# PSUM tiles per stage, and a norm's operands made by quarters, in a two-layer decoder trunk

## The chip, the cores and the metric

The kernel runs on one core of a Trainium2 chip. The time is device microseconds (us) of one execution; the median of several runs is given. The core has engines with a queue each, worked off in order: TensorE (PE in the profile; its weight loads are PEld), VectorE (DVE), ScalarE (ACT), GpSimd (POOL) and SyncE (SP), which issues DMAs. Matmuls write to PSUM, eight banks of 512 fp32 columns over 128 partitions; DVE and ACT read it from there.

## The reference

x has 512 positions and 1024 channels, fp32. Two layers follow each other, each of three sublayers:

```python
x = x + 0.5 * swiglu(rmsnorm(x, ln_ffn1[l]), w_ffn1_gu[l], w_ffn1_down[l])
h = rmsnorm(x, ln_mix[l])
u_pool, q, k, v, gate_logits = jnp.split(h @ w_in[l], splits, axis=-1)
a = pool_mixer(u_pool, pool_w[l], pool_scale[l]) @ w_pool_branch[l]
b = swa_sink_attention(rope(norm(q)), rope(norm(k)), v, sinks[l]) @ w_attn_branch[l]
g_pool, g_attn = jnp.split(jax.nn.sigmoid(gate_logits), 2, axis=-1)
x = x + (g_pool * a + g_attn * b) @ w_out[l]
x = x + 0.5 * swiglu(rmsnorm(x, ln_ffn2[l]), w_ffn2_gu[l], w_ffn2_down[l])
```

(The calls of norm and rope are shortened here.) swiglu(h) is (silu(h Wg) * (h Wu)) Wdown with 2816 hidden columns. The mixer has causal window means of 2, 4, 8 and 16 positions beside attention with 8 query and 2 key heads over a window of 128 positions.

## The kernel before, in words

**Precision.** Every fp32 product is made of three matmuls on fp32r halves: each operand is split into a high half (a cast on ACT) and a low half (source minus high half, on DVE), and `term` issues high x high, high x low, low x high. `split` does this for activations, `Weights` for weights: a weight tile is loaded to `raw`, then `wh` is cast on ACT and `wl` subtracted on DVE. Each call of `W.prep()` after a consumed tile makes the next `wl` (three tiles ahead) and `wh` (four ahead), and sums of weight tiles (five ahead). All engines run in the order of the program text; nothing is reordered by a scheduler.

**Strassen blocks.** A FFN is worked off in three groups of hidden columns (384 + 384, 512 + 512, 512 + 512; the narrow group comes first in the very first FFN and second in the others, so the last one is always wide). Each group has one or two blocks for gate and up, and then one product with the down weights, `down`. Block and down are a Strassen-like scheme (`strassen`, L504) of seven products, named a11, s1, s2, a12, s3, s4, a22. Each adds up in one of three two-bank PSUM tiles: A takes a11, s2, s3 and a22, C takes s1 and s4, Dd takes a12. So A holds a running sum that is read after each of its four products before the next one may add to it. The order is `ORDER` = a11, s1, s2, a12, s3, s4, a22, in the block after a norm `FIRST` = a11, s1, a12, s2, s3, s4, a22. In `down` (L704), the step after each product updates a quarter of x (or two, for a22: row by row) with one DVE operation `x<-mm,x`. Each product has two weight tiles (c = 0, 1) and two halves of rows (q); the weights of s2 and s4 are sums of others.

**Operands of down.** `turned` (L606) transposes the block's results on PE into a fourth two-bank PSUM tile, `turn` (named pt in the profile), and from it makes with ACT and DVE the operands `op` of the seven products, by way of `fa`, `fb` and `fc`. The second block's part t = 1 is turned right after the block; the part t = 0 is held back in `turns` and turned by `flush`, the step after a11 of down. Its result is the operand of a12 and the last term of `fa`, from which a22's operand is made.

**The norm's operand.** The next sublayer's operand is x scaled by the gain (the factor of each row is put on the result), transposed. `Norm.feed(k, pt)` (L375) transposes 128 channels of all 512 positions into one bank, and makes the halves: for a FFN (`halves`) four plain quarters B11, B12, B21, B22 and combinations T1 to T4, for the mixer the plain halves alone. In the last down of a FFN channels 0 to 511 are fed during and after a22 (`mid`), channels 512 to 1023 and the combinations by closures in `pend`, which `due()` runs at fixed points of the next sublayer's first products.

**The mixer.** The tiles A, C and Dd are used bank by bank: `mm()` (L323) hands out the four banks of two of them in turn, for the u, gate and branch products (L1011, L1071); the third holds attention scores (`wide`). The two banks of `turn` take transposes (of heads, of probabilities) and the product with v. Attention, pooling and head norms are generators whose steps stand at fixed half tiles between the u and gate products (`side`, L1006). The gate tile's PSUM is read by `z<-mm,R` on DVE. The out product (L1088) runs over two halves of the channels (d) with four row blocks each.

A tile is the unit of the waits: this shows in the trace, where PE waits for the reader of another bank of the same two-bank tile.

Of the kernel before, what the change touches and what calls it, by code (L numbers as in the profile page):

```python
# [9 lines left out]
F32 = mybir.dt.float32  # L10
# [8 lines left out]
P = 128  # L19
L = 2  # L20
S = 512
# [7 lines left out]
PLACE = {B11: 0, T1: 1, B21: 2, B22: 3}  # L29
OF = {"a11": B11, "s1": T1, "s2": T2, "a12": B21, "s3": T3, "s4": B22, "a22": T4}  # L30
# [77 lines left out]
def trunk(ctx, tc, x0, xT, consts, vecs, rows, w_g4, w_g3, w_d8, w_d6, w_qkv, w_u, w_pool, w_gate, w_br, w_out, out):  # L108
# [6 lines left out]
    pa = pool("pa", 1, space=PSUM)  # L115
# [14 lines left out]
    two = [pa.tile([P, 2, S], F32, name=f"mm{i}") for i in range(3)]  # L130
    turn = pa.tile([P, 2, S], F32, name="pt")
    for _ in range(WARM):
        nc.tensor.matmul(turn[:, 1, :2 * P], warm[:, :P], warm, start=True, stop=True)
# [26 lines left out]
    class Weights:  # L160
# [3 lines left out]
        def __init__(self):  # L164
# [3 lines left out]
            for l in range(L):  # L168
                for f in range(2):
# [9 lines left out]
                    for gi, (at, group) in enumerate(groups(plain)):  # L179
# [9 lines left out]
                        if at:  # L189
                            w = w_d8[l, f, at // 1024]  # L190
                            self.block(lambda h, k, c, w=w: w[h, k, c], (CH, CH), ORDER)
                        else:
                            w = w_d6[l, f]
                            cols = slice(0, CH), slice(CH, 3 * S)
                            self.block(lambda h, k, c, w=w: w[h, k][:, cols[c]], (CH, S), ORDER)

# [149 lines left out]
    class Norm:  # L346
# [15 lines left out]
        def spare(self, j):  # L362
            if j not in self.more:
                self.more[j] = [xl.tile([P, 3 * HT], F32R, name=n, tag=f"{n}{j}") for n in ("th", "tl")]
            return self.more[j]

        def of(self, i, j, n=1):
            if i in PLACE:
                i = PLACE[i]
                return [t[:, i:i + n, j, :] for t in (self.h, self.l)]  # L370
            i -= T2
            return [t.rearrange("p (i t) -> p i t", t=HT)[:, i:i + n, :] for t in self.spare(j)]


        def feed(self, k, pt):  # L375
# [8 lines left out]
            if k < 4:  # L384
                self.keep[k] = xl.tile([P, S], F32, name="keep", tag=f"th{k}")
            xg = self.keep[k] if k < 4 else temp("xg")
            nc.scalar.activation(out=xg, in_=pt, func=AF.Copy, scale=g)
            if k < 4:
                split(*self.of(B11, k), halves(xg)[:, 0:1, :])
                self.first(k, xg)  # L390
            else:
                split(*self.of(B21, k - 4, 2), halves(xg))
                return xg

        def first(self, j, src, scale=None):
            d = temp("d")[:, :HT]
            nc.vector.tensor_tensor(out=d, in0=src[:, :HT], in1=src[:, HT:], op=ALU.subtract)
            split(*self.of(T1, j), halves(d), scale=scale)

        def others(self, j, src, xg, scale=None):  # L400

            t, u = temp("t23"), temp("t4")[:, :HT]
            if scale is None:
                nc.vector.tensor_tensor(out=t[:, HT:], in0=xg[:, HT:], in1=src[:, HT:], op=ALU.subtract)
            else:
                nc.vector.scalar_tensor_tensor(
                    out=t[:, HT:], in0=src[:, HT:], scalar=scale, in1=xg[:, HT:], op0=ALU.mult, op1=ALU.add
                )
            nc.vector.scalar_tensor_tensor(
                out=t[:, :HT], in0=src[:, :HT], scalar=-1.0 if scale is None else scale, in1=t[:, HT:],  # L410
                op0=ALU.mult, op1=ALU.subtract,
# [4 lines left out]
            split(*self.of(T2, j, 2), halves(t))  # L416
            split(*self.of(T4, j), halves(u))

        def split_plain(self, k, b12, src):
            g = self.gain[:, k:k + 1]  # L420
            self.opened()
            if k < 4:
                split(*self.of(B11, k), halves(src)[:, 0:1, :], scale=g)
                split(*(t[:, k:k + 1, :] for t in b12), halves(src)[:, 1:2, :], scale=g)
            else:
                split(*self.of(B21, k - 4, 2), halves(src), scale=g)
# [39 lines left out]
        def spread(self):  # L466
            pr = turn[:, 1, :]
# [5 lines left out]
        def terms(self, w):  # L473
            return pairs(w, [(self.h[:, k, :], self.l[:, k, :]) for k in range(KT)])
# [3 lines left out]
    roles = list(two)  # L478
    pend = []

    def due(n=1):
        for _ in range(n):
            if pend:
                pend.pop(0)()

    @with_exitstack
    def ffn(ctx, nm, nxt, last):
        op = ctx.enter_context(tc.tile_pool(name="op", bufs=3, reuse_waits="tile"))
# [15 lines left out]
        def strassen(order, n, sizes, operand, steps, mid={}):  # L504
# [31 lines left out]
            roles[:] = [Dd, C, A]  # L536
# [694 lines left out]
```

## Time and profile before

| | us |
|---|---|
| median of 3 runs (2042.04 to 2048.88) | 2044.02 |
| profiled execution, whole | 2051.07 |
| its span, first to last instruction | 2049.3 |
| PE busy | 1908.7 (93%) |
| DVE busy | 1461.9 (71%) |
| ACT busy | 1001.5 (49%) |
| mean granted clock of TensorE | 0.971 |

A row of the timeline reads: start, duration, engine, operation, out<-in by the program's names, shape, count, and in brackets the idle time of the engine before it and what ended it. Where a helper records all operations, all have one line (L96 here), so the names of the tiles tell them apart. In a name with several inputs, mm<-wh,op is a matmul into mm of the moving wh and the stationary op. The granted clock is the share of full speed that the throttle let TensorE have; it is either 1 or 0.5 at a time, so 0.96 over a stretch is half clock for 8% of it. Durations of matmuls are modelled and overlap; the distance between their starts is what they cost.

### The profile page before, as it was taken

The page shows a single profiled execution, that of the slowest core. Times are in us where ns is not written, and L with a number is a line of the kernel's source. Part 1 is how long each engine was busy: PE and PEld are TensorE (multiplying, and loading weights), DVE is VectorE, ACT ScalarE, POOL GpSimd, SP SyncE. Part 2 cuts the span into 40 slices and gives each one's busy share as a digit, 9 for nine tenths or more (in the row PEclk, how much of TensorE's full clock was granted, in tenths as well). Part 3 has the DMA queues.
Part 4 walks back from the last instruction along what each step waited for, and adds up shares of the span by engine and source line. Part 5 has one row for each costly group of instructions (what it writes and reads, how often), then busy time and mean ns, then how long its engine had stood idle before and what let it go on. Part 6 is the DMA issues. An engine that isn't in the chain of part 4 may idle for free.

```text
span 2049.3 us, 23932 instructions
## 1 busy us (share of the span) xinstructions
PE 1908.7 (93%) x8928; PEld 1590.7 (78%) x8928; DVE 1461.9 (71%) x1873; ACT 1001.5 (49%) x1457; POOL 124.8 (6%) x152
## 2 busy tenths in 40 slices
PE   9999999878999899999879999998789998999998
PEld 8887887766687678988758897877666786789886
DVE  7877878546454778777877877785555547787877
ACT  6555455344344555555555455553343445545553
POOL 0100100000000000110000111000000000001100
PEclk9999999989999999999989999999999999999999
DMA  7677774211124576676546677742212244666763
GB/s 231 176 210 189 187 188 135 88 62 62 62 83 103 135 178 166 171 213 173 152 117 170 157 182 188 198 144 90 70 51 73 83 103 134 175 161 174 210 180 93
DMA packets 87572, 292.81 MB, mean 143 GB/s; under 512 B 9856, under 2 KB 10112, under 8 KB 87456
## 3 DMA queue, kind: packets, MB, share of 16 engines
q1 hardware_dynamic: 67104, 223.47, 33.0%
q0 software_dynamic: 20208, 67.78, 19.6%
q8 instruction: 70, 1.15, 0.2%
q14 instruction: 46, 0.38, 0.1%
q10 hardware_dynamic: 144, 0.03, 0.0%
HBM read 289.15 MB, written 2.10 MB: 142 GB/s over the span
## 4 chain that ended last, share of the span: by engine, by line
PE 78%; DVE 13%; ACT 6%; issue 3%; DMA 0%; SPq 0%; DVEq 0%; ACTq 0%
PE mm L96 75%; PE pt L96 3%; DVE wl L96 3%; DVE sums L96 1%; ACT wh L96 1%; ACT s L96 1%; DVE x L96 1%; DVE tl L96 1%; ACT xgh L96 1%; ACT op L96 1%; DVE fb L96 1%; ACT sq L96 1%; DVE fa L96 1%; ACT th L96 1%; DVE r L96 1%
## 5 line engine op out<-in xcount | busy, mean ns | idle before, releaser
L96 ACT CAST wh<-raw 128x1024 fp32r<-128x1024 f32 (+3 forms) x443 | 434.4, 988 | 352.7 <-PE mm L96 279.6
L96 DVE TENSOR_TENSOR wl<-raw,wh 128x1024 fp32r<-128x1024 f32 (+3 forms) x443 | 504.5, 1145 | 114.3 <-PE mm L96 88.1
L96 PE MATMUL mm<-wh,op 128*128 128x512 f32 x1232 | 395.4, 399 | 0.0
L96 PE MATMUL mm<-wh,xgh 128*128 128x512 f32 (+2 forms) x904 | 334.8, 370 | 0.0
L96 PE MATMUL mm<-wl,xgh 128*128 128x512 f32 (+2 forms) x904 | 331.9, 367 | 2.0 <-DVE wl L96 1.9
L96 PE MATMUL mm<-wh,xgl 128*128 128x512 f32 (+2 forms) x904 | 331.7, 367 | 0.0
L96 PEld LDWEIGHTS mm<-wh,op 128*128 128x128 f32 x1232 | 237.5, 193 | 49.6
L96 PE MATMUL mm<-wl,op 128*128 128x512 f32 x616 | 244.8, 397 | 1.6 <-DVE wl L96 1.6
L96 PE MATMUL mm<-wl,th 128*128 128x512 f32 (+1 forms) x552 | 211.3, 383 | 14.1 <-DVE wl L96 14.1
L96 PE MATMUL mm<-wh,th 128*128 128x512 f32 (+1 forms) x552 | 211.3, 383 | 12.8 <-ACT u L96 12.5
L96 PE MATMUL mm<-wh,tl 128*128 128x512 f32 (+1 forms) x552 | 210.3, 381 | 0.0
L96 ACT CAST wh<-sums 128x1024 fp32r<-128x1024 f32 (+1 forms) x140 | 137.4, 981 | 129.3 <-DVE sums L96 116.5
L96 PEld LDWEIGHTS mm<-wl,xgh 128*128 128x128 f32 x904 | 170.7, 189 | 25.6 <-DVE wl L96 3.3
L96 DVE TENSOR_TENSOR wl<-sums,wh 128x1024 fp32r<-128x1024 f32 (+1 forms) x140 | 158.2, 1135 | 44.3 <-ACT wh L96 22.0
L96 PEld LDWEIGHTS mm<-wh,xgl 128*128 128x128 f32 x904 | 170.5, 189 | 22.9
L96 PEld LDWEIGHTS mm<-wh,xgh 128*128 128x128 f32 x904 | 170.8, 189 | 22.2
L96 PE MATMUL mm<-xgh,wh 128*128 128x512 f32 x320 | 137.4, 429 | 36.3 <-DVE tl L96 19.4
L96 POOL DMA_DIRECT2D raw<-in_w_g x92 | 79.4, 863 | 1474.0 <-DMA raw<-in_w_g 648.1
L96 PEld LDWEIGHTS mm<-wl,op 128*128 128x128 f32 x616 | 118.8, 193 | 27.5 <-DVE wl L96 3.3
L96 PE MATMUL mm<-xgl,wh 128*128 128x512 f32 x320 | 132.0, 412 | 0.0
L96 PE MATMUL mm<-xgh,wl 128*128 128x512 f32 x320 | 131.6, 411 | 0.0
L96 PEld LDWEIGHTS mm<-wl,th 128*128 128x128 f32 x552 | 106.8, 193 | 31.9 <-DVE wl L96 15.6
(228 smaller groups left out, 2538.6 us busy)
## 6 DMA issues: line engine op xcount, KB each, us to landing
raw<-in_w_g SPq DMA_DIRECT2D x160, 512.0 KB, 4.7
raw<-in_w_d SPq DMA_DIRECT2D x100, 512.0 KB, 4.4
raw<-in_w_g POOLq DMA_DIRECT2D x64, 512.0 KB, 5.9
raw<-in_w_g SPq DMA_DIRECT2D x77, 384.0 KB, 4.0
raw<-in_w_d POOLq DMA_DIRECT2D x40, 512.0 KB, 5.5
raw<-in_w_gate SPq DMA_DIRECT2D x32, 512.0 KB, 3.3
raw<-in_w_g POOLq DMA_DIRECT2D x28, 384.0 KB, 5.3
raw<-in_w_br SPq DMA_DIRECT2D x16, 512.0 KB, 3.3
```

The source lines that it names most:

```text
L96: return lambda *args, **kw: self.tc.keep_in_program_order(call(*args, **kw))
```

## The change

PSUM is now allocated by each stage: a FFN opens three two-bank tiles and `turn` as before, the mixer opens four single banks for `mm()`, one two-bank tile for the scores and two single banks in place of `turn`. The physical banks follow each other as before (`order_`).

In `down` the order is a11, s1, s2, a12, s4, s3, a22, and `flush` runs after s1 instead of after a11. In `turned`, `fa` and `fb` of the second block's part t = 1 read `fc`, the copy in SBUF, instead of PSUM. The operands have fixed places (`AT`) instead of rotating ones.

`feed(q, i, pt)` now makes a quarter-sized piece: 256 channels (q of 4) of 256 positions (i of 2), with eight transposes. ACT scales it in two operations out of PSUM into SBUF, and everything else reads SBUF. In the last down pieces (0, 0) and (1, 0) are fed in s4, (0, 1) and (1, 1) in s3, (2, 1) and (3, 1) in a22; (2, 0) and (3, 0) follow in the next sublayer's first product. In the mixer's out product six of the eight are fed within its second half, whose last two weight tiles are worked off row block by row block (blocks 2 and 3 first), with both their `W.prep()` calls at the end. The mixer's operand lies in another layout, by which u and gate read it in two runs of 256 columns. Its first products are reordered: half of u, half of k and v, the rest of u, the rest of k and v.

```diff
+DOWN = ("a11", "s1", "s2", "a12", "s4", "s3", "a22")
 FIRST = ("a11", "s1", "a12", "s2", "s3", "s4", "a22")
...
+AT = {"a11": 0, "s1": 1, "s2": 2, "s3": 0, "a12": 1, "s4": 2, "a22": 1}
...
-    two = [pa.tile([P, 2, S], F32, name=f"mm{i}") for i in range(3)]
-    turn = pa.tile([P, 2, S], F32, name="pt")
...
+        def feed(self, q, i, pt):
 
             self.opened()
-            for b in range(NB):
-                nc.tensor.transpose(pt[:, b * P:(b + 1) * P], x[:, b, k * P:(k + 1) * P], ident)
-            g = self.gain[:, k:k + 1]
+            for k in range(2):
+                for b in range(2):
+                    at = k * HT + b * P
+                    nc.tensor.transpose(
+                        pt[:, at:at + P], x[:, 2 * i + b, (2 * q + k) * P:(2 * q + k + 1) * P], ident
+                    )
...
+            def scaled(xg):
+                for k in range(2):
+                    cols, n = slice(k * HT, (k + 1) * HT), 2 * q + k
+                    nc.scalar.activation(out=xg[:, cols], in_=pt[:, cols], func=AF.Copy, scale=self.gain[:, n:n + 1])
+                return xg
+
             if not self.halves:
-                split(self.h[:, k, :], self.l[:, k, :], pt, scale=g)
+                split(*(t[:, q, i].rearrange("p k t -> p (k t)") for t in (self.h, self.l)), scaled(temp("xg")))
                 return
...
+            j = q % 2
+            if q < 2 and i == 0:
+                self.keep[0, j] = scaled(self.place(0, 2, j, F32))
+                split(*self.both(B11, j), self.keep[0, j])
+            elif q < 2:
+                self.keep[1, j] = scaled(self.place(0, 0, j, F32))
+                d = temp("d")
+                nc.vector.tensor_tensor(out=d, in0=self.keep[0, j], in1=self.keep[1, j], op=ALU.subtract)
+                split(*self.both(T1, j), d)
+            elif i == 1:
+                xg = scaled(temp("xg"))
+                split(*self.both(B22, j), xg)
+                self.keep[2, j] = t = self.place(1, 0, j, F32)
+                nc.vector.tensor_tensor(out=t, in0=xg, in1=self.keep[1, j], op=ALU.subtract)
+                split(*self.both(T3, j), t)
             else:
...
+                xg, t, u = scaled(temp("xg")), temp("t2"), temp("t4")
+                split(*self.both(B21, j), xg)
+                nc.vector.scalar_tensor_tensor(
+                    out=t, in0=self.keep[0, j], scalar=-1.0, in1=self.keep[2, j], op0=ALU.mult, op1=ALU.subtract
+                )
+                split(*self.both(T2, j), t)
+                nc.vector.scalar_tensor_tensor(out=u, in0=t, scalar=-1.0, in1=xg, op0=ALU.mult, op1=ALU.subtract)
+                split(*self.both(T4, j), u)
...
         def terms(self, w):
-            return pairs(w, [(self.h[:, k, :], self.l[:, k, :]) for k in range(KT)])
...
+            return pairs(w, [[t[:, k // 2, :, k % 2, :] for t in (self.h, self.l)] for k in range(KT)])
...
+        pf = ctx.enter_context(tc.tile_pool(name="pf", bufs=1, space=PSUM, reuse_waits="tile"))
+        three = [pf.tile([P, 2, S], F32, name=f"mm{i}") for i in range(3)]
+        turn = pf.tile([P, 2, S], F32, name="pt")
+        roles = [three[i] for i in order_]
...
-                nc.vector.scalar_tensor_tensor(
-                    out=f["a"], in0=f["a"], scalar=-1.0, in1=pt, op0=ALU.mult, op1=ALU.subtract
-                )
                 f["c"] = fp.tile([P, 2, S], F32, name="fc")[:, :, :n]
                 nc.scalar.copy(out=f["c"], in_=pt)
+                nc.vector.scalar_tensor_tensor(
+                    out=f["a"], in0=f["a"], scalar=-1.0, in1=f["c"], op0=ALU.mult, op1=ALU.subtract
+                )
                 made("s2", f["a"], n)
-                nc.vector.tensor_tensor(out=f["b"], in0=pt, in1=f["b"], op=ALU.subtract)
+                nc.vector.tensor_tensor(out=f["b"], in0=f["c"], in1=f["b"], op=ALU.subtract)
...
-            def a11(pt):
-                add(0, 0, 0.5)(pt)
-                return flush
+            a11 = add(0, 0, 0.5)
 
             def s1(pt):
                 add(1, 1, -0.5)(pt)
                 made("s3", f["b"], n)
+                return flush
...
-                A, _, Dd = roles
-                mid["a22", 0, 1] = lambda: [nxt.feed(i, Dd[:, i, :]) for i in range(2)]
-                mid["a22", 1, 1] = lambda: [nxt.feed(2 + i, turn[:, i, :]) for i in range(2)]
-                pend.extend(stages(nxt, [A[:, 0, :], A[:, 1, :], turn[:, 0, :], turn[:, 1, :]]))
+                Dd = roles[2]
+                for i, (kind, q, t) in enumerate((("s4", 0, 0), ("s3", 0, 1), ("a22", 2, 1))):
+                    for k in range(2):
+                        bank = (Dd, turn)[k][:, 0, :]
+                        mid[kind, k, 1] = lambda q=q + k, t=t, bank=bank: nxt.feed(q, t, bank)
+                pend.extend((lambda bank, q=q: nxt.feed(q, 0, bank)) for q in (2, 3))
...
-                        mid = {("a11", 0, 1): lambda: due(2), ("a11", 1, 1): lambda: due(2), ("s1", 0, 1): due,
-                               ("s1", 1, 1): due, ("a12", 0, 1): due, ("a12", 1, 1): due}
+                        mid = {("a11", k, 1): lambda bank=bank: due(bank[:, 0, :]) for k, bank in ((0, turn), (1, roles[2]))}
...
+        pm = ctx.enter_context(tc.tile_pool(name="pm", bufs=1, space=PSUM, reuse_waits="tile"))
+        ring = {}
+        for i in range(3):
+            n = order_.index(i)
+            if n == 2:
+                wide = pm.tile([P, 2, S], F32, name="sc")
+            else:
+                ring.update((2 - 2 * n + j, pm.tile([P, S], F32, name=f"mm{n}{j}")) for j in range(2))
+        side_bank = [pm.tile([P, S], F32, name=n) for n in ("pt_tp", "pt_pv")]
+        used = [0]
+
+        def mm():
+            used[0] += 1
+            return ring[(used[0] - 1) % 4]
...
-            pt = turn[:, b // 2, :]
+            pt = side_bank[b // 2]
...
-                pk = turn[:, 1, :]
+                pk = side_bank[1]
...
-        for h in range(2):
+
+        def begun(h):
             for i in range(2):
                 for k, t in enumerate(nm.terms(w[i])[4 * h:4 * h + 4]):
                     term(late[i], 4 * h + k, KT, *t)
-                if h == 0:
-                    due(2)
+                if h:
+                    W.prep()
                 else:
-                    if i == 0:
-                        nm.sums()
-                    W.prep()
+                    due(side_bank[i])
+
+        begun(0)
...
+                w_ = W.take("qkv")
...
+                        kt, cols = per * c + k, slice(k * width, (k + 1) * width)
+                        rows = slice(b % 2 * P, (b % 2 + 1) * P)
+                        term(
+                            pts[b], kt, KT, *(t[:, kt // 2, b // 2, kt % 2, rows] for t in (nm.h, nm.l)),
+                            w_[0][:, cols], w_[1][:, cols],
+                        )
+                    if not q and c == 1 and b == 1:
+                        nm.spread(side_bank[1])
                         for i in range(2):
                             pooled(i, late[i])
+                if not q and c == 0:
+                    nm.sums()
+                    praw = temp("praw")
+                    nc.sync.dma_start(out=praw, in_=w_pool[l])
+                    begun(1)
                 if c + 1 < KT // per:
                     W.prep()
-                if not q and c == 0:
-                    praw = temp("praw")
-                    nc.sync.dma_start(out=praw, in_=w_pool[l])
                 if q and c == 1:
                     side(-2)
...
+        sides = [[mm() for _ in range(NB)], [wide[:, 0, :], wide[:, 1, :]]]
+        sides[1] += sides[0][:2]
+        feeds = iter([(q, i) for i in range(2) for q in range(2)] + [(q, 1) for q in (2, 3)])
...
+            for c in range(KT // 2 - 2 * d):
...
+                    part(d, b, c, w)
+                    if d and b % 2:
+                        nxt.feed(*next(feeds), side_bank[b // 2])
                 W.prep()
...
+            if d == 0:
+                for b in range(NB):
+                    added(d, b)
+        w = [W.take("out") for _ in range(2)]
+        for i in (1, 0):
+            for b in (2 * i, 2 * i + 1):
+                for c in range(2):
+                    part(1, b, 2 + c, w[c])
+                if i == 0:
+                    if b == 0:
+                        for n in (2, 3):
+                            added(1, n)
+                    nxt.feed(*next(feeds), side_bank[b])
+        for n in (0, 1):
+            added(1, n)
+        pend.extend((lambda bank, q=q: nxt.feed(q, 0, bank)) for q in (2, 3))
+        W.prep()
+        W.prep()
...
```

More of the change, by code (lines that the diff above doesn't have):

```diff
@@ L128, in trunk @@
     nc.vector.tensor_copy(out=onesr, in_=ones)
-    two = [pa.tile([P, 2, S], F32, name=f"mm{i}") for i in range(3)]
-    turn = pa.tile([P, 2, S], F32, name="pt")
-    for _ in range(WARM):
-        nc.tensor.matmul(turn[:, 1, :2 * P], warm[:, :P], warm, start=True, stop=True)
+    with tc.tile_pool(name="pw", bufs=1, space=PSUM, reuse_waits="tile") as pw:
+        cold = pw.tile([P, S], F32, name="cold")
+        for _ in range(WARM):
+            nc.tensor.matmul(cold[:, :2 * P], warm[:, :P], warm, start=True, stop=True)
     nc.scalar.activation(out=sp.tile([P, 1], F32, name="warm"), in_=ones[:, 0:1], func=AF.Silu)
@@ L375, in feed, with place, slot @@
-        def feed(self, k, pt):
-            self.opened()
-            for b in range(NB):
-                nc.tensor.transpose(pt[:, b * P:(b + 1) * P], x[:, b, k * P:(k + 1) * P], ident)
-            g = self.gain[:, k:k + 1]
+        def place(self, side, i, j, dt=F32R):
+            return xl.tile([P, S], dt, name="more", tag=f"more{side}{i}{j}")
+        def slot(self, i, j):
+            if (i, j) not in self.more:
+                self.more[i, j] = [self.place(side, i, j) for side in range(2)]
+            return self.more[i, j]
@@ L415, in others @@
             )
-            split(*self.of(T2, j, 2), halves(t))
-            split(*self.of(T4, j), halves(u))
+            split(*self.of(T2, j), t[:, :HT])
+            split(*self.of(T3, j), t[:, HT:])
+            split(*self.of(T4, j), u)
         def split_plain(self, k, b12, src):
@@ L473, in terms, with due @@
         def terms(self, w):
-            return pairs(w, [(self.h[:, k, :], self.l[:, k, :]) for k in range(KT)])
-    roles = list(two)
+            return pairs(w, [[t[:, k // 2, :, k % 2, :] for t in (self.h, self.l)] for k in range(KT)])
+    order_ = [0, 1, 2]
     pend = []
[L481 to L484, printed above, removed]
+    def due(bank):
+        if pend:
+            pend.pop(0)(bank)
     @with_exitstack
     def ffn(ctx, nm, nxt, last):
-        op = ctx.enter_context(tc.tile_pool(name="op", bufs=3, reuse_waits="tile"))
+        op = ctx.enter_context(tc.tile_pool(name="op", bufs=1, reuse_waits="tile"))
         fp = ctx.enter_context(tc.tile_pool(name="fp", bufs=1, reuse_waits="tile"))
@@ L774, in ffn @@
         if nm is first:
-            xt = [op.tile([P, 4, S], F32, name="op") for _ in range(2)]
-            acc = op.tile([P, S], F32, name="op")
+            xt = [op.tile([P, 4, S], F32, name="op", tag=f"op{i}") for i in range(2)]
+            acc = op.tile([P, S], F32, name="op", tag="op2")
             later = begin(xt)
@@ L787, in ffn @@
                     elif starts:
-                        mid = {("a11", 0, 1): lambda: due(2), ("a11", 1, 1): lambda: due(2), ("s1", 0, 1): due,
-                               ("s1", 1, 1): due, ("a12", 0, 1): due, ("a12", 1, 1): due}
+                        mid = {("a11", k, 1): lambda bank=bank: due(bank[:, 0, :]) for k, bank in ((0, turn), (1, roles[2]))}
                     block(n, i, FIRST if starts else ORDER, mid)
             down(n, gi == 2)
-    def stages(nm, pts):
-        xg = {}
-        def one(k, pt):
-            xg[k] = nm.feed(k, pt)
-        out = [lambda k=k, pt=pt: one(k, pt) for k, pt in zip(range(4, KT), pts)]
-        if nm.halves:
-            out += [lambda j=j: nm.others(j, nm.keep[j], xg[j + 4]) for j in range(4)]
-        return out
     @with_exitstack
@@ L824, in mix @@
         kT = mp.tile([P, S], F32, name="kT")
-        part_of = lambda k, cols: [t[:, cols] for t in nm.spare(k)]
+        spare = [[nm.place(side, i, j) for side in range(2)] for i, j in ((0, 0), (0, 1), (1, 0), (1, 1), (2, 0))]
+        part_of = lambda k, cols: [t[:, cols] for t in spare[k]]
         kv = mp.tile([P, NB, 4, HD], F32, name="kv")
@@ L1056, in mix @@
             if not q:
-                for g in range(len(WIN)):
-                    split(*part_of(g, slice(S, S + P)), praw[:, g * P:(g + 1) * P])
+                split(*spare[4], praw)
             side(-1 if q else -3)
@@ L1090, in mix @@
         for d in range(2):
-            pts = [t[:, q, :] for t in sides[d] for q in range(2)]
-            for c in range(KT // 2):
-                wh, wl = (t.rearrange("p (k f) -> p k f", k=2) for t in W.take("out"))
+            for c in range(KT // 2 - 2 * d):
+                w = W.take("out")
                 for b in range(NB):
-                    for k in range(2):
-                        kt = 2 * c + k
-                        yh, yl = (t[:, b * P:(b + 1) * P] for t in y[kt])
-                        term(pts[b], kt, KT, yh, yl, wh[:, k, :], wl[:, k, :])
-                    if d == 1 and c < 2 and b % 2:
-                        k = 2 * c + b // 2
-                        nxt.feed(k, turn[:, k % 2, :])
-                W.prep()
```

117 lines of the change are left out of this document (44 added, 73 removed).

## The prediction

> **What bounds the kernel now.** The page was read first, then the list of who waited for whom on TensorE (PE), then the timelines of VectorE (DVE) and PE at the places that this list names, and last the stretches round them.
>
> ```profile
> span 2049.3 us, 23932 instructions
> PE 1908.7 (93%) x8928; PEld 1590.7 (78%) x8928; DVE 1461.9 (71%) x1873; ACT 1001.5 (49%) x1457; POOL 124.8 (6%) x152
> PE 78%; DVE 13%; ACT 6%; issue 3%; DMA 0%; SPq 0%; DVEq 0%; ACTq 0%
> ```
>
> PE is the bound, and idle for 2049.3 - 1908.7 = 140.6 us; no DMA is on the chain. A change that adds no matmul can only win these 140 us and what PE loses at a lower clock after them. In the waits of PE (us in total, times, longest) nearly all of it has names:
>
> ```profile
> PE pt L96 <- DVE fb L96: 35.5, 12, 3.0
> PE mm L96 <- DVE tl L96: 19.4, 6, 8.1
> PE mm L96 <- DVE z L96: 17.7, 14, 2.3
> PE mm L96 <- DVE wl L96: 17.6, 10, 4.3
> PE mm L96 <- ACT u L96: 12.5, 4, 4.0
> PE mm L96 <- DVE xgl L96: 8.5, 4, 2.4
> PE pt L96 <- DVE xgl L96: 6.3, 4, 1.6
> PE pt L96 <- ACT qT L96: 4.6, 2, 2.3
> ```
>
> The first row is one wait in each of the twelve down products. Rows 2, 3 and 8 are the two mixers. The others lie where one sublayer hands x to the next.
>
> **Part 1: single banks in the mixer.** One of the 14 waits for z, in the timelines of DVE and PE:
>
> ```profile
> 507.02 0.68 DVE L96 TENSOR_TENSOR z<-mm,R 128x512 f32<-128x512 f32 x1
> 507.75 0.50 PE L96 MATMUL mm<-xgh,wh 128*128 128x512 f32 x1 [1.83 <-DVE z L96]
> 509.04 0.63 PE L96 MATMUL mm<-xgl,wh 128*128 128x512 f32 x1
> 509.47 0.63 PE L96 MATMUL mm<-xgh,wl 128*128 128x512 f32 x1
> ```
>
> PE is to begin a gate tile whose bank was emptied several tiles ago; it waits until DVE has read the gate tile just before it, the other bank of the same two-bank tile. That 14 of 32 gate tiles wait fits this: every second one shares its tile with the one before. The wait for tl (8.1 us at worst) is the same thing between a pool product and the u tile whose bank it neighbours, that for qT between the two banks of the transposes' tile. With a tile for each bank these waits have no cause: 19.4 + 17.7 + 4.6 = 41.7 us go. What could be late next is the weights' low halves on DVE, since PE no longer gives it those pauses; but DVE has room there:
>
> ```profile
> 444.00:458.00 14.00, 11.68 (x52) 9.15 (x51) 9.12 (x23) 6.82 (x17) 0.00 (x0) 0.88 0.23 76
> 458.00:600.00 142.00, 131.41 (x602) 99.48 (x601) 78.46 (x151) 60.26 (x145) 0.00 (x0) 0.96 0.20 66
> 1458.00:1592.00 134.00, 120.76 (x567) 90.77 (x566) 74.59 (x165) 56.50 (x145) 0.00 (x0) 0.96 0.19 63
> ```
>
> (Columns: stretch, length, busy time of PE, weight loads, DVE, ACT and POOL, granted clock, DMA.) DVE is busy 78.5 of 142 us. The clock column prices the second loss. After the 1.83 us wait the matmuls start 0.43 us apart (509.04, 509.47). Length times missing clock gives 14 x 0.12 + 142 x 0.04 + 134 x 0.04 = 12.7 us, some of it idle time, but the two 8 us waits lie outside these stretches; I take 12 us. The Trainium skill ("TensorE: Matmul & The Clock Gate", HAM oscillation) puts the rule as no PE-idle gaps over about 3.4 us. By it shorter waits cost no clock, and this part would be worth 41.7 us alone; the trace disagrees, with half clock after 1.83 us.
>
> I put back 3 us for waits that then show behind (head transposes that need their rotation on DVE). **Part 1: -41.7 - 12 + 3 = -51 us**; bounds -54, and -17 if two thirds return as waits for data.
>
> The u and gate products now read x in two runs of 256 columns instead of one of 512. No such read is in the trace; the nearest row is the k and v product with 256 columns:
>
> ```profile
> 384.50:389.00 4.50, 4.50 (x40) 4.50 (x40) 2.20 (x3) 1.05 (x1) 0.00 (x0) 1.00 0.43 117
> ```
>
> 37 to 40 matmuls (some straddle the edges) in 4.5 us are 0.113 to 0.122 us each, two of them 0.225 to 0.243 us. Against 0.227 for 512 columns (row below), 2 x 20 tiles x 24 matmuls could lose 0 to 15 us; I take 0, as the sum of columns is the same.
>
> **Part 2: the down product.** The 512-column one at 190 us, DVE's timeline, then one row each of ACT's and PE's, and of the chain of waits:
>
> ```profile
> 193.53 1.21 DVE L96 SCALAR_TENSOR_TENSOR fa<-fa,pt 128x1024 f32<-128x1024 f32 x1
> 196.76 1.23 DVE L96 TENSOR_TENSOR op<-fa,op 128x1024 fp32r<-128x1024 f32 x1 [2.02 <-ACT op L96]
> 197.91 1.22 DVE L96 TENSOR_TENSOR fb<-pt,fb 128x1024 f32<-128x1024 f32 x1
> 199.04 1.22 DVE L96 TENSOR_TENSOR wl<-raw,wh 128x1024 fp32r<-128x1024 f32 x1
> 200.17 1.22 DVE L96 TENSOR_TENSOR sums<-raw 128x1024 f32<-128x1024 f32 x1
> 201.31 1.22 DVE L96 SCALAR_TENSOR_TENSOR x<-mm,x 128x1024 f32<-128x1024 f32 x1
> 203.57 1.21 DVE L96 TENSOR_TENSOR op<-pt,op 128x1024 fp32r<-128x1024 f32 x1
> 227.54 1.23 DVE L96 SCALAR_TENSOR_TENSOR x<-mm,x 128x1024 f32<-128x1024 f32 x1 [1.20 <-PE mm L96]
> 194.77 1.02 ACT L96 COPY fc<-pt 128x1024 f32<-128x1024 f32 x1 [3.75 <-DVE fa L96]
> 199.18 1.09 PE L96 MATMUL pt<-cst,r 128*128 128x128 f32 x8 [2.92 <-DVE fb L96]
> 200.27 39.92 PE mm L96 x176
> 190.00:227.50 37.50, 34.58 (x161) 28.55 (x159) 34.31 (x31) 18.00 (x18) 2.58 (x3) 1.00 0.70 176
> ```
>
> PE takes 39.92 / 176 = 0.227 us a matmul, so 5.45 us for a product of 24. The eight transposes of r wait for fb because both use the tile pt. After the change fa and fb read the copy fc instead, and the transposes stand one product later: this wait, 2.96 us, goes. But DVE is busy 34.3 of these 37.5 us, one operation each 1.135 us. I followed its queue in the new order (each step 1.135 us; ACT's cast before a low half 1.05):
> - fc, fa, cast: DVE waits 1.0 instead of 2.0 us, fb is done at 198.1, the next wl at 199.35, 0.4 us after s1's second half wants it.
> - s1 ends on PE at 201.9, s2 runs from 202.75 (transposes) to 208.2, then a12, whose operand was made two products ahead and now only one. Ahead of its low half in the queue stand x of a11 and s1, s3's low half, four wl and two sums, one of them s4's first, which comes two half products earlier since s4 now precedes s3. It lands at 209.55; PE wants it at 208.65: 0.9 us.
> - s4's first wl stands behind the second s4 sum, x of s2 and s4's low half: 216.4, wanted at 214.8: 1.6 us.
> - **the new wait**: s3 and a22 accumulate in the same bank pair and are now neighbours. a22 may not write before DVE has read s3's sum into x: 0.2 + 1.23 us at the least (the row at 227.54 has DVE idle before it), 1.5 us; s4 stood between them before.
>
> That is 4.4 us against 3.0: +1.4 us. The 384-column ones, where a product is 18 matmuls (4.1 us), come to 5.05 against 3.4 by the same queue: +1.65. Of the nine downs with no norm behind them five are wide and four narrow: 5 x 1.4 + 4 x 1.65 = **+13.6 us**. The half clock after these waits I leave as it is. Bounds: -27 if the new waits are all hidden (9 x 3.0), and +30 if a22 waits as long as a11's x is late now (it ends at 202.53; PE had ended a11 at 199.18 - 2.92 = 196.26: 6.3 us): 9 x (6.3 - 3.0).
>
> **Part 3: the three downs and two mixers that feed a norm.**
>
> ```profile
> L96 ACT ACTIVATE kv<-mm,rstd 128x256 f32<-128x256 f32 x8 | 3.4, 472 | 7.6 <-PE mm L96 7.6
> L96 ACT CAST xgh<-xg 128x512 fp32r<-128x512 f32 x12 | 7.4, 619 | 0.4
> L96 DVE TENSOR_TENSOR xgl<-xg,xgh 128x512 fp32r<-128x512 f32 x12 | 8.3, 692 | 16.6 <-ACT xgh L96 16.6
> 353.00:375.00 22.00, 14.59 (x69) 11.16 (x68) 8.80 (x12) 8.78 (x15) 0.00 (x0) 0.92 0.24 73
> 1015.00:1064.00 49.00, 34.54 (x140) 26.73 (x138) 35.25 (x66) 29.09 (x48) 2.59 (x3) 0.86 0.38 94
> 664.00:712.00 48.00, 37.31 (x149) 29.01 (x149) 34.10 (x57) 26.25 (x38) 2.58 (x3) 0.89 0.51 133
> ```
>
> PE is idle for 22.0 - 14.6 = 7.4 us where x goes to the mixer, 49.0 - 34.5 = 14.5 where a FFN follows a FFN, and 48.0 - 37.3 = 10.7 after the mixer. A piece (256 channels of 256 positions) costs 8 transposes (0.87 us), two scalings of 256 columns on ACT (0.9 in all), one cast (0.62) and one to five DVE operations of 0.69. The transposes are as many as before, and DVE's 22 operations for a FFN's operand (15.2 us) stay. But six of eight pieces move ahead of the hand-over, and each is issued before the x update of the product it sits in, so that update stands behind the piece's chain. In s3: 0.9 + 0.62 + 0.69 + 1.23 = 3.45 us that a22 waits after the transposes (4.1 with the extra difference of a FFN's operand).
> - Into a mixer: 0.4 + 0.9 + 1.6 as above, 0.7 for s4's x, 3.45, and 0.8 for the last pieces' x make 7.85, against 3.0 + 7.4 = 10.4: -2.5, twice.
> - FFN into FFN: 17.0 by the same queue (0.4, 0.9, 1.6, 0.7, 4.1; x of the last pieces 3.05; wl 0.85, 2.15, 1.8; u 1.4) against 2.9 + 14.5 = 17.4: -0.4.
> - Mixer into FFN: the last x waits behind a piece (2.9), then wl 2.0 and 1.9, u 1.3: 8.1 against 10.7: -2.6, twice.
> - Clock: 22 x 0.08, 49 x 0.14, 48 x 0.11 are 1.8, 6.9 and 5.3 us now; I take off a third: -7.
>
> **Part 3: -5 - 0.4 - 5.2 - 7 = -18 us**; bounds -59 (all these waits gone) and +15 (the pieces' chains 3 us longer in each).
>
> **Sum:** -51 + 13.6 - 18 = -55 us. The profiled run took 2051.07 us (span 2049.3) and should take 1996; the median of the runs shown, 2044.02, is 0.3% below it, so 1989 us.
>
> **Rivals.**
> - Down gives its waits up with nothing in their place: DVE's queue is shorter than I count, for instance because fc frees ACT's order. Parts 2 and 3 are then -27 and -25, and some 13 us of half clock go too: 2044 - 51 - 52 = 1941 without them, 1928 with them. For it: DVE's 2.0 us pause at 194.74 to 196.76. Against: DVE is 91% busy there.
> - The mixer's waits return as waits for data, so that part 1 is -17: 2023 us. For it: the longest wait for tl, 8.1 us, needs a DVE that is far behind there. Against: it is busy 78 of the next 142 us.
> - Short waits cost no clock, so that only the idle time itself is won: -41.7 + 3 + 13.6 - 11 = -36, 2008 us. The row at 509.04 is against it. The Trainium skill's rule above speaks for it.
> - Slower: a22's wait for s3's x, in all twelve downs. It decides once it passes about 1.5 + 55 / 12 = 6.1 us each; at 7.5 us the time is 2044 - 55 + 12 x 6 = 2061. For it: x of a11 is 6.3 us late now. Against: by s4 DVE has caught up (227.54).
>
> **Numbers.** Forecast 0.56 (1968 to 2010 by itself), empty downs 0.19, data waits in the mixer 0.11, no clock loss 0.03, slow a22 0.06, something between 0.05. The range runs from 1935 to 2022 and leaves out the slow case and part of the fast one. About 0.3% (6 us) can be told from no change: faster 0.91, same 0.03, slower 0.06.
>
> **What would show it.** In the new profile PE's waits for z, tl and qT are gone, and so is that for fb. Waits of mm for x appear, twelve of about 1.5 us, the three before a hand-over 3 us or more; waits for op and wl in downs come to 1 to 3 us each. If no wait for x shows, part 2 was wrong; if a wait for z stays, part 1; if the gate matmuls start over 0.24 us apart, the split read costs.

## The result and the profile after

The changed kernel takes **1988.45 us** (median of four runs, 1986.74 to 1990.38) where the kernel before took 2045.32 beside it. The ratio is 0.9722, with a 95% interval of 0.9701 to 0.9743. The forecast was 1989.0. Its profiled execution took 1990.38 us, with a span of 1988.4, so the span fell by 60.9 us. From the page of the changed kernel (its helper line is L99 where before it was L96):

```profile
span 1988.4 us, 23898 instructions
PE 1885.0 (95%) x8928; PEld 1566.8 (79%) x8928; DVE 1453.1 (73%) x1829; ACT 1010.1 (51%) x1493; POOL 124.9 (6%) x152
PE 71%; DVE 18%; ACT 6%; issue 3%; DMA 1%; SPq 0%; DVEq 0%; ACTq 0%; POOLq 0%
```

PE is still the bound, with as many matmuls and idle for 103 us instead of 141. DVE's share of the chain grew from 13% to 18%. What PE waits for now (us in total, times, longest):

```profile
PE mm L99 <- DVE wl L99: 37.9, 38, 3.3
PE mm L99 <- DVE x L99: 28.2, 14, 5.5
PE mm L99 <- ACT u L99: 10.4, 4, 3.3
PE mm L99 <- DVE op L99: 9.3, 12, 1.1
PE pt L99 <- DVE x L99: 8.8, 6, 3.4
PE pt_pv L99 <- ACT qT L99: 0.5, 2, 0.2
```

The waits for z, tl and fb are gone, and of qT half a microsecond is left. In their place stand the waits for x and op that the prediction named, and twice as much for wl. Where the 60.9 us came from is read from equal stretches, cut at the same matmuls in both kernels: FFN to mixer, mixer, mixer to FFN, FFN to FFN, then FFN to mixer and mixer in the second layer. A mixer is counted here from its first q product to its first out product; the stretch ahead of it begins with a FFN's last down, and the stretch behind it ends with the next FFN's first down. (The columns are as in the prediction: stretch, length, busy time of PE, weight loads, DVE, ACT and POOL, granted clock, DMA.) Before:

```profile
311.50:392.00 80.50, 70.13 (x358) 58.84 (x357) 54.44 (x68) 35.33 (x51) 1.85 (x3) 0.96 0.39 120
392.00:614.40 222.40, 201.02 (x906) 155.64 (x905) 126.68 (x262) 92.61 (x205) 0.00 (x0) 0.95 0.21 69
614.40:757.60 143.20, 132.25 (x585) 107.07 (x584) 92.81 (x122) 72.06 (x102) 9.49 (x11) 0.96 0.54 137
973.60:1123.00 149.40, 131.77 (x572) 107.05 (x570) 114.51 (x138) 81.09 (x112) 10.35 (x12) 0.93 0.56 148
1340.40:1420.40 80.00, 69.67 (x357) 58.72 (x356) 54.45 (x68) 35.32 (x51) 1.85 (x3) 0.96 0.39 121
1420.40:1640.60 220.20, 199.08 (x906) 154.47 (x905) 126.56 (x262) 92.61 (x205) 0.00 (x0) 0.96 0.21 70
```

After, the same six:

```profile
313.00:389.50 76.50, 68.98 (x357) 57.16 (x356) 53.57 (x68) 40.77 (x67) 1.86 (x3) 0.98 0.41 126
389.50:580.10 190.60, 190.12 (x906) 150.14 (x905) 126.20 (x260) 91.27 (x202) 0.00 (x0) 1.00 0.25 81
580.10:722.70 142.60, 130.79 (x585) 106.35 (x584) 90.47 (x107) 72.57 (x104) 9.49 (x11) 0.98 0.53 137
940.50:1093.00 152.50, 131.50 (x571) 105.48 (x570) 112.28 (x124) 81.20 (x114) 10.36 (x12) 0.94 0.55 145
1310.90:1388.40 77.50, 69.91 (x357) 57.84 (x356) 53.56 (x68) 40.79 (x67) 1.86 (x3) 0.96 0.41 124
1388.40:1579.00 190.60, 190.12 (x906) 150.14 (x906) 126.21 (x260) 91.27 (x202) 0.00 (x0) 1.00 0.25 81
```

The mixers are 31.8 and 29.6 us shorter: PE is idle in them for half a microsecond and runs at full clock. FFN to mixer is 4.0 and 2.5 us shorter, mixer to FFN 0.6 and, in the second layer, which is not shown, 0.9. FFN to FFN is 3.1 us **longer**. That is -61.4 - 8.0 + 3.1 = -66.3 us, and the remaining +5.4 are a remainder: the nine downs without a norm and all that lies between them. PE is idle 5.9 us more there.

### The profile page after: what moved, and what is told of

The parts are those of the page before. It is cut to its first block, busy times and chain, and to the rows that moved or that the text cites. A ratio compares the mean times of both kernels' runs of the same rounds, so it can differ in the third digit from the quotient of the medians.

```text
span 1988.4 us, 23898 instructions
## 1 busy us (share of the span) xinstructions
PE 1885.0 (95%) x8928; PEld 1566.8 (79%) x8928; DVE 1453.1 (73%) x1829; ACT 1010.1 (51%) x1493; POOL 124.9 (6%) x152
## 4 chain that ended last, share of the span: by engine, by line
PE 71%; DVE 18%; ACT 6%; issue 3%; DMA 1%; SPq 0%; DVEq 0%; ACTq 0%; POOLq 0%
PE mm L99 65%; DVE wl L99 5%; DVE x L99 3%; PE sc L99 3%; DVE sums L99 2%; DVE op L99 2%; ACT wh L99 1%; DVE fa L99 1%; PE pt L99 1%; ACT xgh L99 1%; PE pt_pv L99 1%; DMA raw<-in_w_g 1%; ACT xg L99 1%; ACT more L99 1%; DVE t L99 1%
## 5 line engine op out<-in xcount | busy, mean ns | idle before, releaser
L99 ACT CAST wh<-raw 128x1024 fp32r<-128x1024 f32 (+3 forms) x443 | 434.2, 987 | 320.5 <-PE mm L99 244.8
L99 DVE TENSOR_TENSOR wl<-raw,wh 128x1024 fp32r<-128x1024 f32 (+3 forms) x443 | 505.6, 1145 | 119.9 <-PE mm L99 60.7
L99 PE MATMUL mm<-wh,op 128*128 128x512 f32 x1232 | 399.1, 399 | 35.5 <-DVE x L99 26.2
L99 PE MATMUL mm<-wh,more 128*128 128x512 f32 (+1 forms) x1104 | 338.0, 377 | 10.4 <-ACT u L99 10.4
L99 PE MATMUL mm<-wl,xgh 128*128 128x512 f32 (+2 forms) x840 | 312.9, 372 | 15.3 <-DVE wl L99 15.2
L99 PE MATMUL mm<-wh,xgh 128*128 128x512 f32 (+2 forms) x840 | 314.4, 374 | 0.1
L99 PE MATMUL mm<-wh,xgl 128*128 128x512 f32 (+2 forms) x840 | 311.5, 371 | 0.0
L99 PEld LDWEIGHTS mm<-wh,op 128*128 128x128 f32 x1232 | 233.3, 190 | 91.7 <-ACT wh L99 14.4
L99 PE MATMUL mm<-wl,op 128*128 128x512 f32 x616 | 245.8, 399 | 18.4 <-DVE wl L99 18.4
L99 PEld LDWEIGHTS mm<-wh,more 128*128 128x128 f32 x1104 | 208.0, 190 | 42.9 <-ACT u L99 12.0
L99 ACT CAST wh<-sums 128x1024 fp32r<-128x1024 f32 (+1 forms) x140 | 137.4, 982 | 161.7 <-DVE sums L99 142.7
L99 PE MATMUL mm<-wl,more 128*128 128x512 f32 (+1 forms) x552 | 208.5, 378 | 4.2 <-DVE wl L99 4.2
L99 PEld LDWEIGHTS mm<-wl,xgh 128*128 128x128 f32 x840 | 159.3, 190 | 40.6 <-DVE wl L99 19.6
L99 DVE TENSOR_TENSOR wl<-sums,wh 128x1024 fp32r<-128x1024 f32 (+1 forms) x140 | 156.7, 1135 | 41.8 <-ACT wh L99 22.0
L99 PEld LDWEIGHTS mm<-wh,xgl 128*128 128x128 f32 x840 | 159.3, 190 | 21.6
L99 PEld LDWEIGHTS mm<-wh,xgh 128*128 128x128 f32 x840 | 159.2, 189 | 21.4 <-ACT wh L99 0.4
L99 POOL DMA_DIRECT2D raw<-in_w_g x92 | 79.5, 864 | 1415.0 <-DMA raw<-in_w_g 662.9
L99 PEld LDWEIGHTS mm<-wl,op 128*128 128x128 f32 x616 | 117.3, 190 | 52.4 <-DVE wl L99 29.7
L99 PE MATMUL mm<-xgh,wh 128*128 128x512 f32 x320 | 129.5, 405 | 0.0
L99 PE MATMUL mm<-xgh,wl 128*128 128x512 f32 x320 | 125.2, 391 | 0.0
L99 PE MATMUL mm<-xgl,wh 128*128 128x512 f32 x320 | 125.0, 391 | 0.0
L99 DVE SCALAR_TENSOR_TENSOR x<-mm,x 128x1024 f32<-128x1024 f32 (+1 forms) x96 | 103.1, 1084 | 26.2 <-PE mm L99 26.2
```

What stands on the lines that cost most here:

```text
L99: return lambda *args, **kw: self.tc.keep_in_program_order(call(*args, **kw))
```

## The experiments

Every kernel below is the changed kernel with the edit shown; the later ones keep earlier edits, where the text says so. Times are medians, ratios are against the kernel before, run on the same chip.

**Pairs of banks in the mixer again.**

```diff
-ring.update((2 - 2 * n + j, pm.tile([P, S], F32, name=f"mm{n}{j}")) for j in range(2))
-side_bank = [pm.tile([P, S], F32, name=n) for n in ("pt_tp", "pt_pv")]
+pair = pm.tile([P, 2, S], F32, name=f"mm{n}")
+ring.update((2 - 2 * n + j, pair[:, j, :]) for j in range(2))
+side = pm.tile([P, 2, S], F32, name="pt")
+side_bank = [side[:, j, :] for j in range(2)]
```

> The changed kernel with its mixer tiles put back in pairs: four accumulators in two tiles of two banks, and the two side banks as halves of one tile; all else stays. Theory (the mixer's gain is the wait on the neighbouring bank, and the half clock behind it): PE's waits for z, tl and qT come back with about 41 us in all, the two mixers get about 55 us longer, and the time is 1988 + 55 = 2043 us (2030 to 2050). Rival (the gain in the mixer came from something else, for instance norm operands that are ready earlier): under 20 us come back, below 2008 us.

Measured: 2044.06 us, ratio 0.9989 (0.998 to 0.9999). Its waits of PE, and its two mixers between the same matmuls:

```profile
PE mm L99 <- DVE more L99: 19.0, 5, 7.9
PE mm L99 <- DVE z L99: 17.8, 14, 2.3
PE pt L99 <- ACT qT L99: 4.7, 2, 2.3
```

```profile
389.65:609.70 220.05, 198.91 (x907) 154.46 (x906) 126.28 (x259) 92.32 (x202) 0.00 (x0) 0.96 0.21 70
1414.60:1632.75 218.15, 197.01 (x907) 152.96 (x905) 126.15 (x259) 92.21 (x202) 0.00 (x0) 0.97 0.22 70
```

The three waits are back (more is the new name of tl), and the mixers take 438.2 us instead of 381.2. Of these 57.0 us PE is idle for 41.3 more, and 15.7 are the same matmuls taking longer, at a clock of 0.96 and 0.97 instead of 1.00. So the tile's size in banks is the cause of 57.0 of the 61.4 us that the mixers won, nearly all of the waiting among them. (Both kinds of pairs were put back at once, so the share of each is read from the waits alone.) What the matmuls lose lies for the larger part behind short waits. Each mixer has its one long wait, 7.9 us for more, ahead of the first head transposes; up to there the matmuls take 4.7 of the 15.7 us longer. Behind it no wait is longer than 2.4 us, yet PE is busy 166.3 and 163.3 us there against 159.3 in each mixer of the changed kernel: 11.0 us. Length times missing clock gives 7.2 of these (179.6 x 0.03 + 176.6 x 0.01); the cause of the rest is not shown. The rival without clock loss falls. The Trainium skill ("TensorE: Matmul & The Clock Gate", HAM oscillation) warns of PE-idle gaps above about 3.4 us. That covers the two long waits, but not the loss behind the short ones.

**The nine downs: order of products and place of the transposes, two by two.** The old order in the nine downs alone (the weights' plan follows it):

```diff
-    DOWN, S, (2, jn - 2), ...
+    DOWN if final and nxt is not None else ORDER, S, (2, jn - 2), ...
```

> The nine down products that feed no norm get their old order of products back (a12, s3, s4, a22), the weights' plan with them; the late transposes stay after s1, and the copy fc is still read. Theory (a22's wait for x is the price of having s3 and a22 as neighbours, s4's wait for its wl that of s4 coming early): both go, 9 x 1.41 + 5 x 1.28 + 4 x 1.05 = 23 us, the waits for op (7.6 us) stay: 1965 us (1958 to 1972). Rival (DVE's queue is full in these stretches, so a wait only moves to the next product): less than 8 us, over 1980.

The place alone, behind a11 instead of s1 (the operand buffers dealt out to match):

```diff
-a11 = add(0, 0, 0.5)
+def a11(pt):
+    add(0, 0, 0.5)(pt)
+    return flush if early else None
 ...
-    return flush            # in s1
+    return None if early else flush
```

> The new order of products stays in all downs, but in the nine without a norm the transposes of r go back behind a11. Theory: only the waits for op (a12's operand) go, 5 x 0.6 + 4 x 1.14 = 7.6 us; x and wl stay: 1981 us (1977 to 1985). Rival (DVE's queue is the bound): the operand made earlier pushes something else back, and the time stays within 3 us of 1988.

Both:

> As the run with the old order in the nine downs, and the transposes of r go back behind a11, with the operand buffers dealt out to match; only the reads of fc in place of the PSUM tile are left of the change there. Theory (each wait has its own cause in the order): the waits for op, x and wl all go, 31 us, and none comes for fb: 1957 us (1950 to 1965). Rival (DVE's queue is the bound there): under 10 us gained, over 1978.

Measured: order alone **1966.32** us (0.9613, 0.9597 to 0.9629), place alone 1988.62 (0.9719, 0.9705 to 0.9734), both 1966.97 (0.9617, 0.9602 to 0.9631). The order is worth 22 us, the place nothing, with either order. The waits of PE with the order alone, then with the place alone:

```profile
PE mm L99 <- DVE wl L99: 37.7, 38, 3.3
PE mm L99 <- DVE x L99: 15.5, 5, 5.5
PE mm L99 <- DVE op L99: 1.8, 3, 0.6
```

```profile
PE mm L99 <- DVE wl L99: 43.3, 46, 3.3
PE mm L99 <- DVE x L99: 26.8, 13, 5.4
PE mm L99 <- DVE op L99: 1.7, 3, 0.6
```

The total for the order was expected, its make-up was not. The nine waits for x go, 12.7 us, as foretold; but the wait for wl stays, and the wait for op goes, 7.5 us, which was to stay. With the place alone the expectation fails and its rival holds: the time stays within 3 us of 1988. DVE and PE of the changed kernel in the 512-column down, and DVE with the order alone:

```profile
207.06 1.22 DVE L99 TENSOR_TENSOR sums<-sums,raw 128x1024 f32<-128x1024 f32 x1
208.19 1.21 DVE L99 TENSOR_TENSOR op<-pt,op 128x1024 fp32r<-128x1024 f32 x1
...
209.46 0.73 PE L99 MATMUL mm<-wh,op 128*128 128x512 f32 x2 [0.59 <-DVE op L99]
```

```profile
205.18 1.22 DVE L99 TENSOR_TENSOR op<-pt,op 128x1024 fp32r<-128x1024 f32 x1
...
211.98 1.22 DVE L99 TENSOR_TENSOR sums<-sums,raw 128x1024 f32<-128x1024 f32 x1
```

With s4 ahead of s3, the first sum for s4's weights stands on DVE's queue ahead of a12's low half, which lands 1.1 us later for it; with s3 first, that sum comes after it. So the order alone takes the wait for op away. Taking the transposes forward takes it away too (9.3 to 1.7 us), but this gains no time: the wait for wl grows from 37.9 to 43.3 us, and the reading is that the operand made early pushes the weights' low halves back.

**The second piece behind x in the feeding downs.** In a22 the squares of x for the norm move behind both row updates and the piece as well.

```diff
-mid[kind, k, 1] = lambda q=q + k, t=t, bank=bank: nxt.feed(q, t, bank)      # k = 0, 1
+mid[kind, 0, 1] = lambda q=q, t=t, bank=Dd[:, 0, :]: nxt.feed(q, t, bank)
+second[kind] = lambda q=q + 1, t=t: nxt.feed(q, t, turn[:, 0, :])   # called behind add(...)(pt)
```

> The changed kernel, but in the three downs that feed a norm the second piece of each of the products s4, s3 and a22 is issued behind that product's x update instead of ahead of it; nothing else moves. Theory (x stands on DVE's queue behind the piece's chain over ACT, and a22 and the hand-over's transposes wait for it): a22's waits of 4.0, 5.5 and 4.0 us fall to about 1.4 each, the transposes' wait for x after a22 from 3.4 to about 1.5, but the last piece's own chain then ends later: 10 us less in all, 1978 us (1973 to 1983). Rival (the chain is the work to be done before the next sublayer can begin, so what a22 gains comes back as waits behind it): within 3 us of 1988.

Measured: **1975.91** us (0.9657, 0.964 to 0.9674), 12.5 less. ACT, DVE and PE of the changed kernel where a FFN follows a FFN, then DVE and PE with the edit:

```profile
981.78 0.83 ACT L99 ACTIVATE more<-pt,vec 128x256 f32<-128x256 f32 x2
983.42 0.62 ACT L99 CAST xgh<-d 128x512 fp32r<-128x512 f32 x1 [0.81 <-DVE d L99]
...
984.08 0.69 DVE L99 TENSOR_TENSOR xgl<-d,xgh 128x512 fp32r<-128x512 f32 x1 [0.68 <-ACT xgh L99]
984.68 1.22 DVE L99 SCALAR_TENSOR_TENSOR x<-mm,x 128x1024 f32<-128x1024 f32 x1
...
985.95 0.80 PE L99 MATMUL mm<-wh,op 128*128 128x512 f32 x1 [5.48 <-DVE x L99]
```

```profile
975.21 0.69 DVE L99 TENSOR_TENSOR xgl<-d,xgh 128x512 fp32r<-128x512 f32 x1 [0.68 <-ACT xgh L99]
975.82 1.22 DVE L99 TENSOR_TENSOR wl<-raw,wh 128x1024 fp32r<-128x1024 f32 x1
976.95 1.22 DVE L99 SCALAR_TENSOR_TENSOR x<-mm,x 128x1024 f32<-128x1024 f32 x1
...
978.22 0.50 PE L99 MATMUL mm<-wh,op 128*128 128x512 f32 x1 [3.48 <-DVE x L99]
```

s3's x, for which a22 waits, stood behind the chain of the second piece (scaling, difference, cast, low half, going back and forth between ACT and DVE). Without it the wait falls by 2.0 us, not by 4: the first piece's chain and a wl are still ahead of x. The time won does not come back behind the hand-over.

**x ahead of the last piece in the mixer.**

```diff
+    else:
+        for n in (0, 1):
+            added(1, n)
     nxt.feed(*next(feeds), side_bank[b])
-for n in (0, 1):
-    added(1, n)
```

> The changed kernel, but at the end of each mixer the x updates of the two last output tiles are issued ahead of the last piece (3,1) instead of behind it. Theory (the transposes of the next pieces wait 2.4 us for these updates, which stand behind the piece's chain): about 1.3 us go in each of two mixers and nothing comes back, 1985.5 us (1983 to 1987). Rival (the piece's chain is needed as early as x): no difference, within 1 us of 1988.5.

Measured: 1988.91 us (0.9717, 0.9703 to 0.9731), no difference: the rival. In its waits of PE

```profile
PE mm L99 <- DVE wl L99: 38.3, 33, 3.6
PE pt L99 <- DVE x L99: 3.4, 1, 3.4
PE pt L99 <- ACT xg L99: 2.0, 2, 1.0
```

the transposes wait for x only once, where FFN follows FFN. In both mixers they wait 1.0 us for a scaled piece instead of 2.6 us for x, and the wait for wl right behind them is 3.6 us instead of 0.4.

**The three edits in one kernel.**

> The three edits in one kernel: the old order of products in the nine downs without a norm, the second pieces behind x in the feeding downs, x ahead of the last piece in the mixers. Theory (the waits are separate, each with its own cause): the gains add up, 1966 - 10 - 3 = 1953 us (1947 to 1959). Rival (DVE is the bound between the sublayers): no better than the old order alone, 1963 to 1967.

Measured: 1955.44 us (0.9557, 0.9541 to 0.9573). The parts are -22.1, -12.5 and +0.5, which makes 1954.4: the gains add up.

**The weights' sums on GpSimd.**

```diff
-nc.vector.tensor_tensor(out=c["raw"][:, :n], in0=a["raw"][:, :n], in1=b["raw"][:, :n], op=ALU.add)
+nc.gpsimd.tensor_tensor(out=c["raw"][:, :n], in0=a["raw"][:, :n], in1=b["raw"][:, :n], op=ALU.add)
```

> The old order of products in the nine downs without a norm as before, and besides it the sums of the weight tiles (four of them in each down and gate product block) are made on GpSimd instead of VectorE. It measures whether DVE's load sets what is left of the waits for wl and op in the downs and blocks. Theory (DVE is over 90% busy there, and each wait left is a queue that is 0.4 to 1.1 us late): four operations of 1.14 us less per block take the waits for wl away, about 15 us, 1951 us (1945 to 1958). Rival (GpSimd is slower at an add, or slows DVE beside it, so that the sums themselves are late): equal or slower, 1964 us and more.

Measured: **2092.7** us (1.0221, 1.0198 to 1.0244), 126 us slower than with the order alone. The groups of POOL and DVE here (busy us, mean ns, idle before), then DVE's with the order alone:

```profile
L99 POOL TENSOR_TENSOR sums<-raw 128x1024 f32<-128x1024 f32 x52 | 140.8, 2708 | 0.0
...
L99 DVE TENSOR_TENSOR wl<-raw,wh 128x1024 fp32r<-128x1024 f32 x344 | 497.9, 1455 | 89.5 <-PE mm L99 47.5 <-issue 23.5 <-PE sc L99 11.2
```

```profile
L99 DVE TENSOR_TENSOR wl<-raw,wh 128x1024 fp32r<-128x1024 f32 x344 | 418.1, 1218 | 88.9 <-PE mm L99 50.6 <-issue 19.6 <-PE sc L99 11.3
```

A sum takes 2.7 us instead of 1.2, and DVE gets slower beside it (last section); PE's waits for wl grow from 37.7 to 114.9 us. As a way of taking load off DVE it fails, so whether the waits for wl that are left come from DVE's load alone stays open.

**The last pieces in two parts, and both pieces behind x.** On top of the three edits, the operands of s2 and a22 made behind s1's halves:

```diff
 split(*self.both(B21, j), xg)
+def rest(_):        # t, T2, u, T4 as before
+    ...
+pend.append(rest)
 ...
+mid.update({("s1", k, 1): lambda: due(None) for k in range(2)})
```

> The kernel with the three edits together, and in each hand-over to a FFN the last pieces (2,0) and (3,0) are taken in two parts: scaling, cast and low half of the operand of a12 as now, the five operations for the operands of s2 and a22 only behind the halves of s1. Theory (what delays a11's and s1's wl by 4.5 and 3.6 us is the length of the piece's chain on DVE, of which four fifths are needed only two products later): the waits for wl right behind the hand-over fall by 2 to 3 us in each of the three, 1955.4 - 8 = 1947 us (1943 to 1951). Rival (DVE has too much to do until s2 in any order, so that the wait comes at s1, a12 or s2 instead): within 2 us of 1955.4.

And besides, in the feeding downs:

```diff
+if kind == "a22":
+    mid[kind, 0, 1] = pieces.pop(0)
+second[kind] = lambda ps=pieces: [piece() for piece in ps]
```

> As the run with the last pieces in two parts, and besides it both pieces of s4 and of s3 stand behind the x update of their product, not only the second one. Theory (a22's wait of 2.8 to 3.5 us is 1.4 us of the shared bank and the rest the first piece's chain): a22 waits 1.4 us in each of three downs, and 5 us go against the run beside it, 1942 us. Rival (the chains then end later and hold up x of a22 or the hand-over): within 2 us of the run beside it.

Measured: 1958.84 us (0.9571, 0.9558 to 0.9584) and **1949.12** us (0.9523, 0.951 to 0.9536). The waits of PE with the three edits, with the pieces in two parts, and with both behind x:

```profile
PE mm L99 <- DVE wl L99: 42.7, 39, 4.5
PE mm L99 <- ACT u L99: 10.7, 4, 3.5
PE mm L99 <- DVE x L99: 9.1, 3, 3.5
```

```profile
PE mm L99 <- DVE wl L99: 51.3, 40, 5.9
PE mm L99 <- ACT u L99: 4.4, 4, 1.2
```

```profile
PE mm L99 <- DVE x L99: 2.3, 3, 0.8
```

Splitting the pieces gains nothing: 6.3 us less for u, 8.6 more for wl, the rival's picture. Both pieces behind x win 9.7 us by the medians, where 5 were expected; but the two profiled executions are only 5.7 us apart (1954.83 and 1949.17), and this is what the waits explain. a22's three waits fall from 9.1 to 2.3 us together, each below the 1.4 that I took for the least, because the pieces' transposes now run on PE in that time; the transposes' own wait for x grows by 1.8 us. This kernel is 39 us faster than the changed one and 96 faster than the one before.

## Why the prediction was right, and where its terms were not

That the total came out so close (1989.0 against 1988.45) is luck: the main mechanism was right, but errors of opposite sign met in the terms. The measured part 2 is the remainder of the section above.

| term | predicted, us | measured, us |
|---|---|---|
| part 1, mixers | -51 | -61.4 |
| part 2, nine downs | +13.6 | +5.4 |
| part 3, hand-overs | -18 | -4.9 |
| sum, against the profiled run | -55 | -60.9 |

- **Part 1, the waits:** 41.7 less 3 put back, 38.7. Measured: PE is idle 42.5 us before and 1.0 after, 41.5 less. The mechanism is shown by the pairs put back. No wait for data took their place, so the 3 us were too many, and that rival falls.
- **Part 1, the clock: the term that was mis-sized.** I took 12 us; the same 906 matmuls take 10.9 and 9.0 us less of PE's time, 19.9. The step that failed is the stretch: length times missing clock was worked out for 14 + 142 + 134 us. Over the two whole mixers it is 222.4 x 0.05 + 220.2 x 0.04 = 19.9 us. That the two figures are equal is luck again: 4.5 us of the product fall into the two 8 us waits themselves, where hardly a matmul ran to lose time (clock 0.65 over 8.18 us and 0.80 over 7.96), so for about as much of what the matmuls lost the cause is not shown.
- **The split read** at nothing: a mixer of 906 matmuls at 190.12 us leaves no room for a loss. Right.
- **Part 2:** the waits came as named, each smaller: in the 512-column down op 0.6 for 0.9, wl 1.3 for 1.6, x 1.4 for 1.5, and 0.2 for 0.4 at the other wl. "s3 and a22 are now neighbours" was right and is shown by the order put back. The reason for a12's late operand, "made two products ahead and now only one", is half of it: made two products ahead again, its wait goes, but the time stays. With s3 first again, and so without s4's sum ahead of it in the queue, its wait goes too, and only then time is won. The half clock behind the waits for fb, which I left as it is, went (the clock of the remaining stretches was 0.98 to 0.99 and is 1.00), but PE's busy time in them fell by only 0.5 us; why is not shown.
- **Part 3, into a mixer:** -2.5 us of waiting each. Measured: PE idle 10.4 and 10.3 us before, 7.5 and 7.6 after. Right.
- **Part 3, FFN into FFN: the wrong sign.** I had 17.0 us of waiting against 17.4; PE is idle 21.0 against 17.6. a22's x was 4.1 and is 5.5, u was 1.4 and is 3.3, the last pieces' x 3.05 and 3.4 to 3.6. The step that failed is that the update "stands behind the piece's chain", counted as the sum of one piece's operations: the chains of both pieces stand ahead of s3's x, each goes from ACT to DVE, back to ACT and back to DVE, and a cast of a weight tile and a wl lie in between.
- **Part 3, mixer into FFN:** 8.1 us of waiting against 10.7 before; PE is idle for 11.8 us of the stretch shown, against 11.0 before. The waits for wl and u were too small in the same way.
- **Part 3, the clock:** -7 us taken, but FFN to FFN only went from 0.93 to 0.94, and the others from 0.96 to 0.96 or 0.98; PE's busy time in the five falls by 3.3 us. Waits of 3 us and more are still there.
- **The slow case** (a22 at 7.5 us in all twelve downs): 1.4 us in nine, 4 to 5.5 in three. It stayed far from its 6.1 us.

## What to carry to other kernels

Give each PSUM bank that is emptied by itself a tile of its own: two-bank tiles cost 55 us of 2044 here, a quarter of it as matmuls that took longer behind the waits. Before an operation is put into an in-order queue, look at what stands behind it and who waits for that: an x update behind a chain over two engines cost 12 us of the gain, and an order of products that makes one wait for the x update before it and puts an operand behind a sum needed later cost 22. Putting either right took no work away. Where a queue is nearly full, making one operand earlier can only make another late, as the place alone did here.

## What the runs showed of the hardware

Beside an add on GpSimd, DVE's operations with both operands in SBUF get longer, up to some three times. With the sums on GpSimd:

```profile
210.85 2.68 POOL L99 TENSOR_TENSOR sums<-raw 128x1024 f32<-128x1024 f32 x1
...
210.68 3.95 DVE L99 TENSOR_TENSOR fb<-fc,fb 128x1024 f32<-128x1024 f32 x1
```

With the order alone fb<-fc,fb takes at most 1.22 us; here it takes 3.95 and ends 1.1 us after the add that began beside it. The x updates, which read one operand from PSUM, keep their mean of 1083 ns in both kernels. The Trainium skill ("SBUF — State Buffer", Who interferes with whom) states this: a DVE instruction with two SBUF inputs contends with a GpSimd instruction that reads SBUF. The traces agree.
